# Two loads in the middle of a hybrid decoder block issued later, and one transposed tile evacuated earlier

## The chip, the cores and the metric

The kernel runs on one NeuronCore of a Trainium2 chip. The metric is the device time of one execution in microseconds. Before the change three runs took 972.06, 972.55 and 972.64 us, median 972.55 us. TensorE does the matrix products (PE in the profile, PEld its weight loads), VectorE and ScalarE the elementwise work (DVE, ACT), GpSimd a part of it (POOL). SyncE (SP; its instruction stream is SPq) issues most of the DMAs.

## The reference

One decoder block on 1024 tokens plus 16 meta tokens, width 1024, all in float32:

```
h   = concat(meta_tokens, x)
mix = mixer(rms_norm(h, pre_mix_norm))        # two causal convolution groups, then w_out
h   = h + rms_norm(mix, post_mix_norm)
xn  = rms_norm(h, pre_ffn_norm)
ff  = (silu(xn @ w_gate) * (xn @ w_up)) @ w_down     # 1024 -> 2816 -> 1024
out = (h + rms_norm(ff, post_ffn_norm))[16:]
```

The change lies where the mixer's output projection ends and the first products of `xn @ w_gate` and `xn @ w_up` begin.

## The kernel before

**Arithmetic.** A float32 operand is split into a rounded high part and the rest, its low part, and a product of two operands is made of three matmuls (`mm3`, lines 107 to 109: high by high, high by low, low by high; 512 columns each). So each matmul operand needs a cast on ACT (the high part) and a subtraction on DVE (the low part) before PE can use it.

**Output projection.** The mixer's output has eight row tiles of 128 tokens. `group` (quoted below) multiplies them by `w_out` in three groups: tiles 0 to 2, 3 to 5, then 6 and 7. Each group runs over the eight blocks of `w_out`, and between the blocks it calls the steps of a table, `at`. `norms` then makes of a group the new hidden state `h` (stored to DRAM as `hd`) and the normalised rows `hn`.

**Turning the tiles.** The FFN needs `hn` with channels on the partitions. Tiles 0 to 4 are turned by a DVE block transposition (`send`, line 675), a store to DRAM (`xd`, line 676), a load back in another order (`fetch`, line 681, four DMAs), and copies on ACT (`receive`, lines 689 to 691; `back(i)` calls it for tile i). Tiles 5, 6 and 7 are transposed on PE into two PSUM banks (`turn`, line 668, tile `pt`) and copied out by ACT (line 670). The result lies in four quadrants `raw`. `raw[0, 0]` holds tokens 0 to 511 and channels 0 to 511; its high and low parts are `B11h` and `B11l`, complete once tile 3 has been received.

**FFN.** The gate and up products are made in pairs (`Pair`) of weight blocks. A pair needs seven products of half size in place of eight; (j, n) is product n of pair j. The first ones are (0, 1), (1, 1), (0, 2), (1, 2), (0, 6), (1, 6), and (0, 1) and (1, 1) use `B11`, (j, 2) use `B21`, (j, 6) use `T2`. The weights of pair j arrive by `Pair.load` (line 746) in tiles `u`; in the program's full names `u110` is pair 1, up weights, first block. Their split parts are the tiles `op` (high: line 716 on ACT; low: line 703 on DVE). PSUM banks are handed out by hand: product (0, 1) takes banks 5 and 6, which the PE transposition of tile 5 used just before.

**What sets the order.** The whole program is ordered by hand: every engine executes in the order in which the source calls it, and SP issues its DMAs in that order too. A DMA that waits holds all DMAs behind it on SP. What it waits for is the data it moves, and the buffer it writes: `u110` lies in the ring `tp`, in the buffer that held `hn` of tile 5, so it may be loaded once PE has transposed tile 5. The other first blocks lie in the ring `wp`, in buffers that held blocks 5, 6 and 7 of `w_out` (tiles `ws_o`); these are free when DVE has made the low part of that block (line 168).

**Around the change.** During the group of tiles 6 and 7 the table calls `step1` to `step4` and, ahead of the last two blocks of `w_out`, `early`. `step1` calls `norms` for tiles 3 to 5 and sends tile 3, `step2` fetches it, `step3` sends tile 4, `early` receives tile 3, transposes tile 5 on PE and makes the operands of the products (0, 1) and (1, 1). `residual_x` (line 636) loads 128 rows of x, which `norms` adds for tiles 6 and 7.

Of the kernel before, what the change touches and what calls it, by code (L numbers as in the profile page):

```python
# [54 lines left out]
def hybrid_block(ctx: ExitStack, tc: tile.TileContext, xT, x, w_first, w_in, w_out, w_gate, w_up, w_down, par, g_post, g_ffn, g_out, out):  # L55
# [39 lines left out]
    def big(name, dt=F32R, pool=None):  # L95

        return (pool or xg).tile([P, 4 * HALF], dt, tag="x", name=name)
# [4 lines left out]
    def blocks(t):  # L102
        return t[:, : 4 * HALF].rearrange("p (a b) -> p a b", a=4)
# [52 lines left out]
    def split_o(k, eng=None):  # L156
        split_o_hi(k)
        split_o_lo(k, eng)

    def split_o_hi(k):  # L160
        if k in (3, 4):
            wu[k] = [held[k - 3][:, q, :] for q in range(2)]
        else:
            wu[k] = [wp.tile([P, D], F32R, tag=t, name=f"{t}_o{k}") for t in ("wh", "wl")]
        nc.scalar.copy(wu[k][0], raw_w["o", k])
# [468 lines left out]
    def residual_x(i):  # L634
        h = hp.tile([P, D], F32, tag="h", name=f"h{i}")
        nc.sync.dma_start(h, x[i * P : (i + 1) * P, :])
        return h

    def norms(grp, left, s1, hs, between=None, first=None, parts=False):
        n_ = len(grp)  # L640
        v = sm.tile([P, 16], F32, tag="s2", name=f"pm{grp[0]}")
        nc.vector.tensor_tensor(v[:, :n_], s1[:, 0:n_], s1[:, 4 : 4 + n_], op=ALU.add)
        r = rsqrt_n(v[:, :n_], 1.0 / D, RMS_EPS, n_, f"pm{grp[0]}")
        if first:
            first()
        v2 = sm.tile([P, 16], F32, tag="s2", name=f"pf{grp[0]}")
        n = {}
        for q, i in enumerate(grp):
            nc.vector.scalar_tensor_tensor(hs[i], left[i], r[:, q : q + 1], hs[i], op0=ALU.mult, op1=ALU.add)
            n[i] = row(tp, "t", f"hn{i}", TT)[:, :D]  # L650
            nc.scalar.activation(n[i], hs[i], AF.Square, accum_out=v2[:, q : q + 1])
            nc.sync.dma_start(hd[i], hs[i])
        if between:
            between()
        r = rsqrt_n(v2[:, :n_], 1.0 / D, RMS_EPS, n_, f"pf{grp[0]}")
        last = [lambda q=q, i=i: nc.vector.scalar_tensor_tensor(n[i], hs[i], r[:, q : q + 1], gB["ffn"], op0=ALU.mult, op1=ALU.mult) for q, i in enumerate(grp)]
        if parts:
            return n, last
        for f in last:
            f()  # L660
        return n

    def turn(i, n, at=(0, 1)):
        c = slice((i % 4) * P, (i % 4 + 1) * P)
        for q in range(2):
            pt = bank(at[q], f"pt{i}_{q}")
            for k in range(4):
                nc.tensor.transpose(pt[:, k * P : (k + 1) * P], n[:, (4 * q + k) * P : (4 * q + k + 1) * P], ident)
            p4 = pt.rearrange("p (a b) -> p a b", a=4)
            nc.scalar.copy(raw[q, i // 4][:, :, c], p4)  # L670
# [7 lines left out]
    def fetch(i, n):  # L678
        for j in range(4):
            src = xd[i].rearrange("(i r) (j x) -> j r i x", i=4, j=4)[j]  # L680
            nc.sync.dma_start(n[32 * j : 32 * j + 32].rearrange("r (i x) -> r i x", i=4), src)

    def receive(i, n):
        c = slice((i % 4) * P, (i % 4 + 1) * P)
        split4 = lambda t: t[:, :, c].rearrange("p k (i q) -> p k i q", i=4)
        for q in range(2):
            n4 = n.rearrange("p (i k q) -> p k i q", i=4, k=8)[:, 4 * q : 4 * q + 4]
            if q == 0 and i < 4:
                nc.scalar.copy(split4(B11[0]), n4)
                nc.vector.tensor_tensor(split4(B11[1]), n4, split4(B11[0]).bitcast(F32), op=ALU.subtract)  # L690
            nc.scalar.copy(split4(raw[q, i // 4]), n4)
# [10 lines left out]
    def sub(o, a, b, eng=None):  # L702
        (eng or nc.vector).tensor_tensor(o, a, b, op=ALU.subtract)  # L703
# [25 lines left out]
    class Pair:  # L729
# [19 lines left out]
        def a_side(self, n, m):  # L749
            a11, a12 = self.u[m, 0][:, :512], self.u[m, 0][:, 512:]  # L750
            if n not in (1, 2):
                a21, a22 = self.u[m, 1][:, :512], self.u[m, 1][:, 512:]
            if n == 1:
                s = a11
            elif n == 6:
                add(a21, a21, a22)
                sub(a11, a21, a11)
                s = a11
            elif n == 2:
                s = a12  # L760
            elif n == 5:
                s = a21
            elif n == 7:
                sub(a21, a22, a11)
                s = a21
            elif n == 3:
                sub(a12, a12, a11)
                s = a12
            else:
                s = a22  # L770
            return s
# [124 lines left out]
    hs = {i: residual_x(i) for i in (0, 1, 2)}  # L896
    pairs = {j: Pair(j) for j in range(3)}
# [10 lines left out]
    def turns(*grp, at=(0, 1)):  # L908
        return lambda: [turn(i, hn.pop(i), at if q or len(grp) == 1 else (0, 1)) for q, i in enumerate(grp)]

    def back(i):
        return lambda: receive(i, hn.pop(i))

    hs = {i: residual_x(i) for i in (3, 4, 5)}
# [57 lines left out]
    def turned(i):  # L972
        send(i, hn[i], big(f"xt{i}", F32, rp)[:, :D])
# [5 lines left out]
    def step1():  # L979
        n, muls = norms((3, 4, 5), left, s1, hs, between_5, lambda: split_o_hi(5), True)  # L980
        hn.update(n)
        pairs[1].load(0, (1,))
        muls[0]()
        turned(3)
        hn_muls.extend(muls[1:])
# [8 lines left out]
    def step3():  # L994
        split_o(7)
        pairs[1].load(0, (0,))
        turned(4)
        for i in (6, 7):
            hs[i] = residual_x(i)

    def step4():
        X[2] = pair("B21", (rp, rp))
# [2 lines left out]
    def b21_hi(c):  # L1005
        nc.scalar.copy(X[2][0][:, :, c], raw[1, 0][:, :, c])

    def b21_lo(c):
        sub(X[2][1][:, :, c], raw[1, 0][:, :, c], X[2][0][:, :, c].bitcast(F32))

    def early():
        for q in range(2):
            raw[q, 1] = blocks(big(f"raw{q}1", F32))
        a_side(0)
        b21_lo(slice(0, 3 * P))
        back(3)()
        b21_hi(slice(3 * P, 4 * P))
        b21_lo(slice(3 * P, 4 * P))
        turns(5, at=(5, 6))()
        fetch(4, hn[4])  # L1020
        a_side(1, (hp, "h"), (jp, "jk"))

    hn_muls = []
    s1, left = group((6, 7), up, {1: step1, 2: step2, 3: step3, 4: step4, 6: early})
    r11, r21, r12, r22 = raw[0, 0], raw[1, 0], raw[0, 1], raw[1, 1]
    T2r = blocks(big("T2r", F32))
# [404 lines left out]
```

## Time and profile before

| | |
|---|---|
| median of three runs | 972.55 us |
| the profiled execution: its own time | 972.49 us |
| its span (first to last instruction) | 970.7 us |
| mean granted TensorE clock | 0.993 |
| PE busy | 955.0 us, 98% |
| DVE busy | 713.6 us, 74% |
| ACT busy | 406.5 us, 42% |
| POOL busy | 249.6 us, 26% |

The difference between the execution's own time and its span, 1.8 us, lies around the instructions. PE is busy nearly throughout, so what is worth reading is where it is not. The views used below are the list of waits (who waited for whom, in total, how often, the longest), the chain of work that ended last, timelines of single engines (start, duration, what was done, and in brackets the idle time before it), tables by stretch with the granted clock, and the DMA issues with the time from issue to landing. Matmuls are pipelined: each row shows 0.39 us, but they start 0.23 us apart at the full clock.

### The profile page before, as it was taken

The numbers are of one execution on the slowest core, as the hardware profiler recorded it, in microseconds if no ns is written. First come the engines' busy times: TensorE is split into PE (matmuls) and PEld (weight loads), VectorE is DVE, ScalarE is ACT, GpSimd is POOL, SyncE is SP. The second block draws the span as 40 slices with busy tenths as digits, with TensorE's granted clock in tenths as the row PEclk, the third lists the DMA queues.
The fourth block names the chain that finished last, engine by engine and source line by source line (L and its number), as shares of the span: only waits on it lengthen the run. The fifth ranks groups of instructions, "written<-read, shape, count | busy, mean of one in ns | idle before, by whom it ended". The sixth has DMA issues, their size and how long they took to land.

```text
span 970.7 us, 12488 instructions
## 1 busy us (share of the span) xinstructions
PE 955.0 (98%) x4554; PEld 821.1 (85%) x4554; DVE 713.6 (74%) x1030; ACT 406.5 (42%) x666; POOL 249.6 (26%) x219
## 2 busy tenths in 40 slices
PE   9999999999999699999999999999999999999997
PEld 9999999998888588888888888888888888888885
DVE  7699999886467599997866876777765653546776
ACT  8533423465436473453443343443433333322341
POOL 1277945542000000004134132141240311112210
PEclk9999999999999799999999999999999999999999
DMA  8011111214356630464532623534319999866866
GB/s 309 23 44 63 47 44 44 65 44 163 121 180 231 211 115 1 184 241 161 217 131 109 238 109 131 187 127 163 147 31 343 321 329 376 261 186 200 321 209 245
DMA packets 62317, 161.92 MB, mean 167 GB/s; under 512 B 6576, under 2 KB 10160, under 8 KB 62256
## 3 DMA queue, kind: packets, MB, share of 16 engines
q1 hardware_dynamic: 45792, 109.08, 31.0%
q0 software_dynamic: 11088, 40.38, 12.9%
q10 hardware_dynamic: 5376, 11.67, 3.3%
q8 instruction: 36, 0.59, 0.3%
q14 instruction: 25, 0.20, 0.1%
HBM read 109.72 MB, written 51.38 MB: 166 GB/s over the span
## 4 chain that ended last, share of the span: by engine, by line
PE 98%; DMA 1%; ACT 0%; DVE 0%; SPq 0%; issue 0%; DVEq 0%; ACTq 0%
PE x L107 8%; PE x L109 8%; PE x L108 8%; PE y L107 6%; PE y L109 6%; PE y L108 6%; PE qx L109 4%; PE qx L108 4%; PE qx L107 4%; PE qy L108 3%; PE qy L109 3%; PE qy L107 3%; PE po L107 3%; PE po L109 3%; PE po L108 3%; PE p_v L108 2%
## 5 line engine op out<-in xcount | busy, mean ns | idle before, releaser
L716 ACT CAST op<-u 128x512 fp32r<-128x512 f32 x154 | 93.5, 622 | 190.4 <-DVE u L703 96.2
L703 DVE TENSOR_TENSOR op<-u,op 128x512 fp32r<-128x512 f32 x154 | 118.1, 808 | 48.6 <-ACT op L716 48.6
L703 DVE TENSOR_TENSOR db<-wb,db 128x512 fp32r<-128x512 f32 x77 | 54.9, 716 | 85.3 <-ACT db L1236 85.0
L706 POOL TENSOR_TENSOR C<-C,C 128x512 f32<-128x512 f32 x9 | 15.5, 1722 | 372.2 <-DMA gdA<-U 208.2
L1236 ACT CAST db<-wb 128x512 fp32r<-128x512 f32 x77 | 47.2, 620 | 116.3 <-PE qx L109 55.6
L108 PE MATMUL qx<-db,a 128*128 128x512 f32 x176 | 68.6, 390 | 0.0
L107 PE MATMUL qx<-db,a 128*128 128x512 f32 x176 | 68.6, 390 | 0.0
L109 PE MATMUL qx<-db,a 128*128 128x512 f32 x176 | 68.5, 389 | 0.0
L700 DVE TENSOR_TENSOR U<-y,U 128x512 f32<-128x512 f32 x66 | 43.1, 683 | 17.8 <-PE y L109 17.8
L108 PE MATMUL qy<-db,a 128*128 128x512 f32 x132 | 51.5, 390 | 0.0
L109 PE MATMUL qy<-db,a 128*128 128x512 f32 x132 | 51.4, 390 | 0.0
L107 PE MATMUL qy<-db,a 128*128 128x512 f32 x132 | 51.4, 390 | 0.0
L1109 POOL DMA_DIRECT2D a<-gdS x44 | 23.2, 528 | 91.6 <-PE qx L109 46.0
L706 POOL TENSOR_TENSOR U<-U,U 128x512 f32<-128x512 f32 x17 | 28.2, 1658 | 60.2 <-ACT U L831 46.5
L107 PE MATMUL x<-B11h,op 128*128 128x512 f32 x88 | 35.4, 402 | 8.0 <-ACT raw L670 8.0
L388 DVE SCALAR_TENSOR_TENSOR ae<-d,pr,ae 128x512 f32<-128x512 f32 x56 | 42.0, 750 | 0.0
L388 DVE SCALAR_TENSOR_TENSOR ac<-g,pr,ac 128x512 f32<-128x512 f32 x56 | 42.0, 750 | 0.0
L108 PEld LDWEIGHTS qx<-db,a 128*128 128x128 f32 x176 | 33.1, 188 | 6.9
L107 PEld LDWEIGHTS qx<-db,a 128*128 128x128 f32 x176 | 33.0, 188 | 6.9
L109 PEld LDWEIGHTS qx<-db,a 128*128 128x128 f32 x176 | 33.1, 188 | 6.8
L108 PE MATMUL x<-B11l,op 128*128 128x512 f32 x88 | 35.2, 400 | 0.0
L109 PE MATMUL x<-B11h,op 128*128 128x512 f32 x88 | 35.2, 400 | 0.0
(358 smaller groups left out, 2914.3 us busy)
## 6 DMA issues: line engine op xcount, KB each, us to landing
a<-gdS POOLq DMA_DIRECT2D x44, 512.0 KB, 4.0
a<-gdA POOLq DMA_DIRECT2D x33, 512.0 KB, 5.6
u<-w_gate_u SPq DMA_DIRECT2D x22, 512.0 KB, 4.9
u<-w_up_u SPq DMA_DIRECT2D x22, 512.0 KB, 5.8
gdS<-HI SPq DMA_DIRECT2D x44, 256.0 KB, 2.3
gdA<-HI SPq DMA_DIRECT2D x33, 256.0 KB, 2.0
gdS<-GS SPq DMA_DIRECT2D x33, 256.0 KB, 2.6
ws_o<-w_out_u SPq DMA_DIRECT2D x14, 512.0 KB, 4.6
```

The lines of the kernel that those rows point to most:

```text
L107: nc.tensor.matmul(o, lh, rh, start=start, stop=False, skip_group_check=again)
L108: nc.tensor.matmul(o, lh, rl, start=False, stop=False, skip_group_check=again)
L109: nc.tensor.matmul(o, ll, rh, start=False, stop=stop, skip_group_check=again)
L388: nc.vector.scalar_tensor_tensor(out if i == n - 1 else acc, src[:, i : i + HALF], w(i), init if i == first else acc, op0=ALU.mult, op1=AL ...
L700: (eng or nc.vector).tensor_tensor(o, a, b, op=ALU.add)
L703: (eng or nc.vector).tensor_tensor(o, a, b, op=ALU.subtract)
L706: (eng or nc.vector).tensor_tensor(o, a, b, op=ALU.mult)
L716: nc.scalar.copy(t[:, 0, :], src)
L1109: nc.gpsimd.dma_start(loads[n, j], gd[an][j])
L1236: nc.scalar.copy(t[:, 0, :], b)
```

## The change

Two issues on SP and two copies on ACT change places. No instruction is added, removed or resized.

- `pairs[1].load(0, (1,))`, the load of `u110`, goes from `step1` to `early`, behind the transposition of tile 5.
- The two loads of rows of x for tiles 6 and 7 go from `step3` to the place behind that.
- The transposition of tile 5 with its copies, `turns(5, ...)`, goes ahead of `back(3)`, which receives tile 3.

```
     def step1():
         n, muls = norms((3, 4, 5), left, s1, hs, between_5, lambda: split_o_hi(5), True)
         hn.update(n)
-        pairs[1].load(0, (1,))
         muls[0]()
...
     def step3():
...
         turned(4)
-        for i in (6, 7):
-            hs[i] = residual_x(i)
...
     def early():
...
         b21_lo(slice(0, 3 * P))
+        turns(5, at=(5, 6))()
+        pairs[1].load(0, (1,))
+        for i in (6, 7):
+            hs[i] = residual_x(i)
         back(3)()
         b21_hi(slice(3 * P, 4 * P))
         b21_lo(slice(3 * P, 4 * P))
-        turns(5, at=(5, 6))()
         fetch(4, hn[4])
         a_side(1, (hp, "h"), (jp, "jk"))
```

The DMAs on SP from the first weight load of pair 0 to the fetch of tile 4, before (u000, u010, u100, u110 are weight blocks: pair, gate 0 or up 1, block; xd3 and hn3 are tile 3 on its way to DRAM and back; h6 and h7 rows of x):

```order
L746 DMA u000_2862<-w_gate_u 128x1024
L746 DMA u110_2873<-w_up_u 128x1024
L676 DMA xd3_2262<-xt3_2876 128x1024
L746 DMA u010_2895<-w_up_u 128x1024
L681 DMA hn3_2850<-xd3_2262 32x4x256 x4
L746 DMA u100_2919<-w_gate_u 128x1024
L676 DMA xd4_2263<-xt4_2921 128x1024
L636 DMA h6_2924<-x_tok 128x1024
L636 DMA h7_2926<-x_tok 128x1024
L681 DMA hn4_2854<-xd4_2263 32x4x256 x4
```

The same DMAs after the change:

```order
L746 DMA u000_2862<-w_gate_u 128x1024
L676 DMA xd3_2262<-xt3_2874 128x1024
L746 DMA u010_2893<-w_up_u 128x1024
L681 DMA hn3_2850<-xd3_2262 32x4x256 x4
L746 DMA u100_2917<-w_gate_u 128x1024
L676 DMA xd4_2263<-xt4_2919 128x1024
L746 DMA u110_2982<-w_up_u 128x1024
L636 DMA h6_2984<-x_tok 128x1024
L636 DMA h7_2986<-x_tok 128x1024
L681 DMA hn4_2854<-xd4_2263 32x4x256 x4
```

Only u110 has moved, from second place to seventh; h6 and h7 stand behind xd4 as they did, now with u110 ahead of them.

ACT, from the operands of product (0, 1) to the first square of the group of tiles 6 and 7, before (pt5 is tile 5 in PSUM, op_1_jm the high parts for product (j, 1)):

```order
L716 CAST op_1_00_2969<-u000_2862 128x512
L716 CAST op_1_01_2971<-u010_2895 128x512
L689 CAST B11h_2552<-hn3_2850 128x4x128
L691 COPY raw00_2554<-hn3_2850 128x4x128
L691 COPY raw10_2555<-hn3_2850 128x4x128
L1006 CAST B21h_2940<-raw10_2555 128x4x128
L670 COPY raw01_2967<-pt5_0_2982 128x4x128
L670 COPY raw11_2968<-pt5_1_2988 128x4x128
L716 CAST op_1_10_2998<-u100_2919 128x512
L716 CAST op_1_11_3000<-u110_2873 128x512
L628 ACTIVATE sq60_3030,s1_6_3028<-po60_2818 128x512
```

After the change:

```order
L716 CAST op_1_00_2963<-u000_2862 128x512
L716 CAST op_1_01_2965<-u010_2893 128x512
L670 COPY raw01_2961<-pt5_0_2970 128x4x128
L670 COPY raw11_2962<-pt5_1_2976 128x4x128
L689 CAST B11h_2552<-hn3_2850 128x4x128
L691 COPY raw00_2554<-hn3_2850 128x4x128
L691 COPY raw10_2555<-hn3_2850 128x4x128
L1003 CAST B21h_2934<-raw10_2555 128x4x128
L716 CAST op_1_10_2998<-u100_2917 128x512
L716 CAST op_1_11_3000<-u110_2982 128x512
L628 ACTIVATE sq60_3030,s1_6_3028<-po60_2818 128x512
```

The two copies out of PSUM (L670) stand ahead of the four rows that receive tile 3. On PE, DVE and POOL the rows stand in the order in which they stood before.

More of the change, by code (lines that the diff above doesn't have):

```diff
@@ L981, in step1 @@
         hn.update(n)
-        pairs[1].load(0, (1,))
         muls[0]()
@@ L997, in step3 @@
         turned(4)
-        for i in (6, 7):
-            hs[i] = residual_x(i)
     def step4():
@@ L1015, in early @@
         b21_lo(slice(0, 3 * P))
+        turns(5, at=(5, 6))()
+        pairs[1].load(0, (1,))
+        for i in (6, 7):
+            hs[i] = residual_x(i)
         back(3)()
@@ L1018, in early @@
         b21_lo(slice(3 * P, 4 * P))
-        turns(5, at=(5, 6))()
         fetch(4, hn[4])
```

## The prediction

> **What bounds the kernel now.** PE is busy for 98% of the span, so I read its list of waits first (total us, how often, the longest):
>
> ```profile
> PE x L107 <- ACT raw L670: 8.0, 1, 8.0
> PE warm L89 <- DVE pr L113: 1.1, 1, 1.1
> ```
>
> The second is at the program's start. In the first, ahead of the first matmul of product (0, 1), PE stands for 8.0 us, and the copy of the transposed tile 5 out of PSUM releases it. The chain of work that ended last shows what led there (start, duration, what):
>
> ```profile
> 317.99 5.61 DMA xd<-xt
> ...
> 324.98 3.09 DMA hn<-xd
> 328.17 0.62 ACT B11h L689
> 328.79 1.05 ACT raw L691 x2
> 329.86 0.62 ACT B21h L1006
> 330.48 0.49 ACT raw L670
> 331.02 0.80 PE x L107
> ```
>
> Tile 3 leaves for DRAM at 317.99, comes back, and ACT receives it; only then does ACT copy tile 5, whose banks product (0, 1) takes. Tile 5 was transposed by 317.6, so its copy is late only because it stands behind tile 3 in ACT's order. Why tile 3 left so late is on SP, in its timeline and its waits from 307 to 326:
>
> ```profile
> 308.12 0.33 SPq L746 DMA_DIRECT2D u<-w_gate_u  x1
> 317.61 0.33 SPq L746 DMA_DIRECT2D u<-w_up_u  x1
> ...
> 318.51 0.38 SPq L746 DMA_DIRECT2D u<-w_up_u  x1
> 323.66 1.75 SPq L681 DMA_DIRECT2D hn<-xd  x4
> 325.51 0.38 SPq L746 DMA_DIRECT2D u<-w_gate_u  x1
> ```
> ```profile
> SPq L746 <- DVE hn L656: 6.8, 1, 6.8
> ...
> SPq L746 <- PE pt L668: 2.3, 1, 2.3
> ```
>
> After u000 (308.12) SP issues nothing until u110 at 317.61: 6.8 us until DVE has normalised tile 5, and 2.3 more until PE has transposed it, which frees u110's buffer. Behind u110 waits the store of tile 3, which DVE had ready long before:
>
> ```profile
> 310.48 1.25 DVE L675 STREAM_TRANSPOSE xt<-hn 128x1024 f32<-128x1024 f32 x1
> 311.65 1.18 DVE L168 TENSOR_TENSOR wl_o<-ws_o,wh_o 128x1024 fp32r<-128x1024 f32 x1
> ...
> 316.28 1.24 DVE L675 STREAM_TRANSPOSE xt<-hn 128x1024 f32<-128x1024 f32 x1
> ```
>
> Ready at 311.73, issued at 317.99: the stall begins there. Its price needs the last matmul ahead of it, the first of product (0, 2) behind it, 48 matmuls at full speed for comparison, and the clock (third number from the end of a stretch's row):
>
> ```profile
> 322.64 0.39 PE L109 MATMUL po<-wh_o,ybl 128*128 128x512 f32 x1
> ```
> ```profile
> L107 PE MATMUL x<-B21h,op x16: 389/390/479, 344.5 to 356.5; 128*128 128x512 f32 x16
> ```
> ```profile
> 400.66 0.39 PE L107 MATMUL x<-T4h,op 128*128 128x512 f32 x1
> ...
> 411.54 0.39 PE L107 MATMUL x<-B11h,op 128*128 128x512 f32 x1
> ```
> ```profile
> 324.00:326.00 2.00, 0.00 (x0) 0.00 (x0) 0.49 (x1) 0.62 (x1) 0.00 (x0) 1.00 0.48 154
> 326.00:328.00 2.00, 0.00 (x0) 0.00 (x0) 1.87 (x2) 0.00 (x0) 0.00 (x0) 0.51 0.98 207
> ...
> 336.00:338.00 2.00, 2.00 (x10) 1.60 (x9) 1.77 (x5) 1.69 (x5) 0.00 (x0) 0.93 0.04 11
> ```
>
> The 48 matmuls of (0, 4) and (1, 4) take 411.54 - 400.66 = 10.88 us, 0.227 each. So PE could begin (0, 1) at 322.64 + 0.23 = 322.87 and (0, 2), 48 matmuls later, at 333.75. It begins (0, 2) at 344.5. **The stall costs 10.75 us in all**: 331.02 - 322.87 = 8.15 of standing and 2.6 of matmuls at half clock until the clock is back at about 336.
>
> **The change, part by part.** First what tile 3 gains. The times from issue to landing, in the stretch 303 to 312, where one transfer follows another, and then in two busier ones (317 to 326, 325 to 336):
>
> ```profile
> hd<-h SPq DMA_DIRECT2D x3, 512.0 KB, 2.7
> u<-w_gate_u SPq DMA_DIRECT2D x1, 512.0 KB, 3.8
> ```
> ```profile
> xd<-xt SPq DMA_DIRECT2D x2, 512.0 KB, 5.9
> hn<-xd SPq DMA_DIRECT2D x4, 128.0 KB, 2.9
> ```
> ```profile
> h<-x_tok SPq DMA_DIRECT2D x2, 512.0 KB, 7.8
> ```
>
> And the making of B11's low part:
>
> ```profile
> 328.82 0.69 DVE L690 TENSOR_TENSOR B11l<-hn,B11h 128x512 fp32r<-128x512 f32 x1 [0.95 <-ACT B11h L689]
> ```
>
> *Tile 3's way.* With u110 out of the way SP issues the store at 311.8. It lands between 2.7 us later (the stores of h, also SBUF to DRAM) and 5.9 (the sends as they were, among loads): 314.5 to 317.7. I take 314.5, since only u010 goes out beside it; u010 waits for the low part of block 6, at 311.65 + 1.18 = 312.83, and lands at 316.7 (3.8) to 318.8 (5.9). The four fetches take SP 1.75 us, and the last, issued about 1.3 us behind the first, lands 2.9 us on: 314.5 + 1.3 + 2.9 = 318.7, at the slow end 321.9. ACT has the high part of product (0, 1) and its partner by then, and copies tile 5 out of PSUM ahead of tile 3, in time in which it would wait for tile 3. So B11h stands at 319.3 (318.7 + 0.62), the low part 0.7 later, at 320.0, against 322.87 when PE asks. *Without cover* the two copies would cost their 1.05 us. At the slow end B11h is ready at 322.5 and the low part at 323.2, needed by the second matmul at 323.1: a wait of 0.1. So the 8.15 us go, and with them the 2.6 of half clock.
>
> *What is late next: u110 itself.* SP reaches it behind the store of tile 4 (DVE ready at 316.28 + 1.24 = 317.52, 0.4 us to issue) at 318.0, 0.4 later than before, and it now stands behind u100 and that store. PE wants it only for the second half of (1, 1), at 322.87 + 36 x 0.227 = 331.0. But ACT works in order, and behind the cast of u110 stand the squares of tiles 6 and 7, which begin the whole normalisation; DVE follows ACT. These rows show the old times:
>
> ```profile
> 332.38 0.61 ACT L628 ACTIVATE sq<-po 128x512 f32<-128x512 f32 x1
> ...
> 340.91 1.05 ACT L803 COPY U<-x 128x512 f32<-128x512 f32 x2
> ...
> 353.61 1.22 ACT L930 CAST T2h<-T2r 128x512 fp32r<-128x512 f32 x2
> ```
> ```profile
> 355.30 1.29 DVE L703 TENSOR_TENSOR T2l<-T2r,T2h 128x512 fp32r<-128x512 f32 x2
> ```
> ```profile
> 357.14 1.98 PE L784 MATMUL y<-T2h,op 128*128 128x512 f32 x8
> 358.96 1.07 PE L784 MATMUL y<-T2l,op 128*128 128x512 f32 x4
> ```
>
> Product (0, 2) accumulates in the bank that the copy at 340.91 empties; half of its 1.05 us, 341.4, against 344.5 gives 3.1 us of room. Product (0, 6) needs the last T2h, at 353.61 + 1.22 = 354.83, at 357.14: 2.3 us, the tightest place; T2l, at 356.59, has 2.4. So PE can come forward by at most 2.3 us more than the ACT and DVE work does. That work comes forward by 332.38 less the new time of the first square, which is the landing of u110 plus 0.62 us of cast, and no earlier than 323.0, the end of PE's group.
>
> - u110 lands after 3.8 us (the load with the queue to itself), at 321.8: squares at 323.0, forward by 9.4, and PE gets all 10.75.
> - After 7.8 (the loads of x, which stood behind three transfers), at 325.8: squares at 326.4, forward by 6.0, PE by 8.3.
> - I take 5.9, the row of the sends, which also stood behind one or two transfers of that size: 323.9, squares at 324.5, forward by 7.9, PE by 7.9 + 2.3 = 10.2.
>
> *The rest costs nothing.* h6 and h7 go out at about 318.4 and 319; even after 7.8 us they are there at 326.8, when the four squares that begin at 324.5 end (0.6 each), and DVE adds them only after that. The fetch of tile 4 follows its store by itself. u010 and u100, issued at 318.5 and 325.5 before, come some 6 and 9 us earlier. If u010's landing were late, the cast of its part would hold the copies behind it; at 318.8 it is still ahead of tile 3's slow arrival.
>
> **Sum.** 972.49 (the profiled execution; the median of the runs, 972.55, is 0.06 above it) - 10.2 = **962.3 us**. Behind this stage PE works without a wait to the end, so an earlier PE ends earlier by as much.
>
> [...] The clock still stood at 1.00 in the stretch 324 to 326 and fell in the next, some 3 us into the wait. [...]
>
> **The rivals.**
>
> - *A late u110.* Its landing is at the far end or beyond, since the fetch of tile 3, u100, the store of tile 4 and it crowd the engines. For: loads of x took 7.8. Against: these stood among fetches of small pieces too. PE waits at (0, 2) or (0, 6), and gains 7.5 to 9.5: 963 to 965, about 964.3.
> - *Tile 3 is still late.* If store and fetch slow each other with u010, a part of the wait stays at 322.87. It does so once the fetch lands beyond 321.8 (0.62 + 0.69 ahead of 323.1); a rest of 3.2 us with half clock behind it costs 5.8 and leaves 4.9, 967.6. For: the sends took 5.9. Against: between 312 and 316 nothing else would be moving.
> - *The store does not move.* If something else than u110 held it, only ACT's order changes: PE starts after B11l, at 328.82 + 0.69 = 329.5 in place of 331.02, and the time is near 971.0. For: a store can wait for its own semaphore. Against: its data were ready at 311.73 and SP's waits name u110's buffer.
> - *Slower.* The order on ACT makes u110 the gate of the normalisation. Once it lands at 334.1 or later, the squares begin more than 2.3 us behind their old time and the gain is gone and more: landing at 336 puts them at 336.6, 4.2 behind, less the room of 2.3, and 1.9 is lost, 974.4. For: the gate is real. Against: 16 us in flight would be double the slowest transfer here.
>
> **How the numbers follow.** The forecast, 961.7 to 963, has 0.68; a late u110 0.16; a late tile 3 0.07; the unmoved store 0.05; slower 0.04. The range is 961.3 to 965.0: its low end is the whole 10.75 with 0.4 for the spread of runs (972.06 to 972.64), its high end takes in the late u110; some 0.15 is left out. A run tells 0.2%, 1.9 us, from no change. Faster by more than that: 0.68 + 0.16 + 0.07 = 0.91. Within: 0.05. Slower: 0.04.
>
> **What would show it.** The store of tile 3 on SP at 311.8; no wait of PE at (0, 1), or under 0.5 us; a clock of 1.00 from 324 on; (0, 2) at about 333.8; the first square between 323 and 325; and if PE waits anywhere, at (0, 2) or at (0, 6) for T2h, by some tenths. A wait of over 2 us at either, or SP silent until 317.6, would prove the forecast wrong.

## The result, and the profile after

| | before | after |
|---|---|---|
| median of the runs | 972.55 us (972.0 to 972.64) | 963.06 us (962.42 to 963.29) |
| the profiled execution: its own time | 972.49 us | 963.29 us |
| its span | 970.7 us | 961.5 us |
| mean granted TensorE clock | 0.993 | 0.999 |

The ratio after to before is 0.9903, with an interval of 0.9888 to 0.9917: 9.5 us faster, where 10.2 were forecast. The median is 0.8 us above the predicted time: inside the range of 961.3 to 965.0, and 0.06 above the upper end of the forecast's own 961.7 to 963, where the rival "A late u110" begins. One execution of the changed kernel, the profiled one of its repeat further down, ran at a granted clock of 0.851 and took 1054.83 us; it is left out of every comparison.

The list of PE's waits, whole (total us, how often, the longest):

```profile
PE warm L89 <- DVE pr L113: 1.1, 1, 1.1
PE p_g L108 <- DVE xl L185: 0.4, 1, 0.4
PE y L784 <- ACT T2h L930: 0.2, 1, 0.2
PE p_g L287 <- ACT xh L182: 0.2, 1, 0.2
```

The wait of 8.0 us ahead of product (0, 1) is gone. In this stage only the third row is left: 0.2 us ahead of (0, 6), for the last `T2h`; the two of `p_g` lie in the program's first 10 us. SP's timeline shows why the long wait is gone (start, duration, what):

```profile
311.89 0.32 SPq L676 DMA_DIRECT2D xd<-xt  x1
313.00 0.33 SPq L746 DMA_DIRECT2D u<-w_up_u  x1
314.70 1.75 SPq L681 DMA_DIRECT2D hn<-xd  x4
316.54 0.38 SPq L746 DMA_DIRECT2D u<-w_gate_u  x1
317.68 0.34 SPq L676 DMA_DIRECT2D xd<-xt  x1
318.11 0.86 SPq L746 DMA_DIRECT2D u<-w_up_u  x1
319.02 1.41 SPq L636 DMA_DIRECT2D h<-x_tok  x2
323.28 1.76 SPq L681 DMA_DIRECT2D hn<-xd  x4
```

Tile 3 leaves at 311.89 instead of 317.99, and u110 (the L746 row at 318.11) no longer stands ahead of it. PE's timeline has the last matmul of the output projection, the first of (0, 1), of (0, 2) and the last ahead of (0, 6), and the first of (0, 6):

```profile
323.16 0.39 PE L109 MATMUL po<-wh_o,ybl 128*128 128x512 f32 x1
323.39 0.39 PE L107 MATMUL x<-B11h,op 128*128 128x512 f32 x1
...
334.40 0.50 PE L107 MATMUL x<-B21h,op 128*128 128x512 f32 x1
...
347.13 0.39 PE L109 MATMUL x<-B21h,op 128*128 128x512 f32 x1
347.74 2.12 PE L784 MATMUL y<-T2h,op 128*128 128x512 f32 x8 [0.23 <-ACT T2h L930]
```

(0, 1) follows the projection without a gap. One thing has to be taken out of these times first. The projection now ends at 323.16, 0.52 us later than before (322.64), though nothing ahead of it changed; in the ten profiles compared here it ends between 322.64 and 323.78. So kernels are compared below by a stretch that starts there, from the last matmul of the projection to the first of (0, 6). **Before it is 357.14 - 322.64 = 34.50 us, after it 347.74 - 323.16 = 24.58**: 9.92 us are gained in the stage. Without any wait it would be 11.11 to (0, 2), as the prediction worked out (333.75 - 322.64), and from there the 12.64 of before (357.14 - 344.5): 23.75. The stage is 0.83 above that, more than the 0.23 of the row in brackets. That row counts from the end of the matmul ahead, 0.39 us behind its start, though the next one could start 0.23 behind it. By the starts, (0, 6) is 0.38 late (347.74 against 347.13 + 0.23), and (0, 2) is 0.13 late (334.40 against 323.39 + 10.88), for the copy that empties its bank; the other 0.32 lies behind that gap: the 24 matmuls of (0, 2) take 5.59 us (5.44 before), the 16 transpositions on PE 1.79 (1.66), and the 24 matmuls of (1, 2) 5.58 (5.54).

What is left shows on ACT, in its timeline, and in the chain that ended last, cut to this stage:

```profile
320.87 0.62 ACT L689 CAST B11h<-hn 128x512 fp32r<-128x512 f32 x1 [1.51 <-DVE B21l L703]
...
324.49 0.62 ACT L716 CAST op<-u 128x512 fp32r<-128x512 f32 x1 [0.79 <-DMA u<-w_up_u]
325.02 0.59 ACT L628 ACTIVATE sq<-po 128x512 f32<-128x512 f32 x1
...
330.31 1.15 ACT L691 COPY raw<-hn 128x512 f32<-128x512 f32 x2 [0.65 <-DMA hn<-xd]
...
346.47 1.22 ACT L930 CAST T2h<-T2r 128x512 fp32r<-128x512 f32 x2 [1.19 <-DVE T2r L703]
```
```profile
317.68 5.53 DMA xd<-xt
...
324.61 5.60 DMA hn<-xd
...
330.31 1.15 ACT raw L691 x2
...
346.47 1.23 ACT T2h L930 x2
...
347.74 1.43 PE y L784 x5
```

From 323 on ACT stands twice for a transfer: 0.79 us for u110, ahead of the squares, and 0.65 us for tile 4 coming back from DRAM (the L691 row). The chain ends on the second: store of tile 4, fetch, the copies, the normalised rows, `T2h`, PE. The prediction had followed u110 and counted tile 4 at nothing.

### The profile page after: what moved, and what is told of

The parts are those of the page before. It is cut to its first block, busy times and chain, and to the rows that moved or that the text cites. A ratio compares the mean times of both kernels' runs of the same rounds, so it can differ in the third digit from the quotient of the medians.

```text
span 961.5 us, 12487 instructions
## 1 busy us (share of the span) xinstructions
PE 952.9 (99%) x4554; PEld 818.9 (85%) x4554; DVE 713.5 (74%) x1030; ACT 406.5 (42%) x666; POOL 251.2 (26%) x219
## 4 chain that ended last, share of the span: by engine, by line
PE 93%; DVE 3%; DMA 2%; ACT 1%; issue 1%; SPq 0%; DVEq 0%; ACTq 0%
PE x L107 8%; PE x L109 8%; PE x L108 8%; PE y L107 6%; PE y L109 6%; PE y L108 6%; PE qx L108 4%; PE qx L109 4%; PE qx L107 4%; PE qy L108 3%; PE qy L109 3%; PE qy L107 3%; PE po L107 2%; PE po L109 2%; PE po L108 2%; PE p_c L107 2%
## 5 line engine op out<-in xcount | busy, mean ns | idle before, releaser
L107 PE MATMUL x<-B21h,op 128*128 128x512 f32 x88 | 34.5, 392 | 0.0
L109 PE MATMUL x<-B21h,op 128*128 128x512 f32 x88 | 34.3, 390 | 0.0
L108 PE MATMUL x<-B21l,op 128*128 128x512 f32 x88 | 34.3, 390 | 0.0
```

The source lines that it names most:

```text
L107: nc.tensor.matmul(o, lh, rh, start=start, stop=False, skip_group_check=again)
L108: nc.tensor.matmul(o, lh, rl, start=False, stop=False, skip_group_check=again)
L109: nc.tensor.matmul(o, ll, rh, start=False, stop=stop, skip_group_check=again)
```

## The experiments

Each of the eight variants stands beside the kernel before, timed on the same chip as it (median 973.15 us, for loads_sorted 973.33). Diffs are against the changed kernel. "Wait" is PE's longest in the stage; "half clock" is worked out from the rows by 2 us, as shown further down; "none" is a granted clock of 1.00 in every 2 us from 322 to 350 in the changed kernel, and in the five others matmuls that start 0.22 to 0.24 us apart, but for the first behind a gap or a transposition, in the rows looked at (322 to 334 and 346 to 358). The six kernels with ratios of 0.9895 to 0.9903 can't be told apart by their times: what is said of their differences rests on one profile of each, and how much the stretch of one kernel varies between profiles was not measured.

| kernel | stretch, us | wait, us | half clock, us | median, us | ratio (interval) |
|---|---|---|---|---|---|
| before | 34.50 | 8.0 at (0, 1) | 10.2 | | |
| changed kernel | 24.58 | 0.2 at (0, 6) | none | 963.06 | 0.9903 (0.9888 to 0.9917) |
| turn_only | 33.62 | 7.1 at (0, 1) | 6.8 | 971.31 | 0.998 (0.9972 to 0.9989) |
| loads_only | 24.91 | 0.4 at (0, 1) | none | 963.43 | 0.9898 (0.9885 to 0.9912) |
| x_rows_first | 29.04 | 3.4 at (1, 1) | 3.4 | 966.57 | 0.9932 (0.9919 to 0.9946) |
| up_last | 30.89 | 4.1 at (1, 1) | 6.8 | 968.39 | 0.9952 (0.9939 to 0.9964) |
| half_behind | 24.97 | 0.4 at (0, 2) | none | 963.35 | 0.9898 (0.9884 to 0.9913) |
| rows_behind | 25.03 | 0.4 at (0, 2) | none | 963.48 | 0.9901 (0.9887 to 0.9916) |
| all_three | 23.76 | none | none | 962.79 | 0.9896 (0.988 to 0.9913) |
| loads_sorted | 24.82 | 0.2 at (0, 6) | none | 963.42 | 0.9895 (0.9878 to 0.9911) |

### Which half of the change carries the gain

**turn_only** leaves the loads where they were and makes only the new order of tile 5 on ACT:

```
     def step1():
...
         hn.update(n)
+        pairs[1].load(0, (1,))
         muls[0]()
...
     def step3():
...
         turned(4)
+        for i in (6, 7):
+            hs[i] = residual_x(i)
...
         turns(5, at=(5, 6))()
-        pairs[1].load(0, (1,))
-        for i in (6, 7):
-            hs[i] = residual_x(i)
         back(3)()
```

> Kernel before, with the second half of the change alone: the transposition of tile 5 and its two copies ahead of the reception of tile 3, all loads at their old places. My theory (the store of tile 3 waits on SP behind u110, and that is the stall): the store still goes at about 318.0, PE still waits at product (0, 1), only until the low part of B11 (329.5 in place of 331.02), so 1.5 us less, and the squares come 1.0 us earlier: 970.5 to 971.3 us. Rival (the order on ACT carries the gain, since the copy of tile 5 released PE): 963 to 965 us.

SP's timeline and PE's waits of turn_only:

```profile
318.06 0.33 SPq L746 DMA_DIRECT2D u<-w_up_u  x1
318.45 0.42 SPq L676 DMA_DIRECT2D xd<-xt  x1
```
```profile
PE x L107 <- ACT B11h L689: 7.1, 1, 7.1
```

The store of tile 3 stays behind u110, and PE waits 7.1 us, now for `B11h` itself. This is the rival "The store does not move", worked out as a gain of 1.5 us. By the medians on this chip it is 1.84 (973.15 and 971.31), by the stretches of the two profiles 0.88; the runs of turn_only spread from 970.2 to 972.64.

**loads_only** does the other half: the loads move, the turn of tile 5 stays behind tile 3.

```
+        back(3)()
+        b21_hi(slice(3 * P, 4 * P))
+        b21_lo(slice(3 * P, 4 * P))
         turns(5, at=(5, 6))()
         pairs[1].load(0, (1,))
         for i in (6, 7):
             hs[i] = residual_x(i)
-        back(3)()
-        b21_hi(slice(3 * P, 4 * P))
-        b21_lo(slice(3 * P, 4 * P))
         fetch(4, hn[4])
```

> The changed kernel, with tile 5 transposed and copied behind the reception of tile 3 as in the kernel before: the moved loads alone. My theory: tile 3 is received from 320.9 on as in the changed kernel, the copies of tile 5 come at 323.1 to 324.1 behind it, so PE waits 0.3 us at product (0, 1) at about 323.4, its clock stays at 1.00, and the squares move by 0.2 us: 963.0 to 963.6 us, within 0.5 us of the changed kernel. Rival (the copies belong to the cause): PE stands for 1 us or more, 964.5 us or later.

PE's waits of loads_only in the stage:

```profile
PE x L107 <- ACT raw L670: 0.4, 1, 0.4
PE y L784 <- ACT T2h L930: 0.2, 1, 0.2
```

The wait for the copy of tile 5 is there again, but 0.4 us long instead of 8.0. The moved loads carry nearly all of the gain; the order on ACT is worth 24.91 - 24.58 = 0.33 us of the stretch, too little for the times to tell. That it is u110 among the moved loads, and not the rows of x, shows in x_rows_first below: there the rows keep their old place, and the wait at (0, 1) is gone all the same.

### Where a later u110 would bite

**x_rows_first** sends the two rows of x ahead of u110 again; **up_last** sends u110 behind the fetch of tile 4. In both u110 lands later and nothing else is added.

```
     def step3():
...
         turned(4)
+        for i in (6, 7):
+            hs[i] = residual_x(i)
...
         pairs[1].load(0, (1,))
-        for i in (6, 7):
-            hs[i] = residual_x(i)
```
```
         turns(5, at=(5, 6))()
-        pairs[1].load(0, (1,))
         for i in (6, 7):
             hs[i] = residual_x(i)
...
         fetch(4, hn[4])
+        pairs[1].load(0, (1,))
```

> The changed kernel, with the two loads of rows of x back at their old place, behind the store of tile 4 and so ahead of u110. My theory (the landing of u110 is the gate: ACT casts it ahead of the squares, DVE follows, PE waits at (0, 6) for T2h): u110 lands at 327 to 328.4 in place of 324.47, the squares begin that much later, 0.65 us of it is taken up by a wait for tile 4 that ACT has now, and PE waits 2 to 3 us more at (0, 2) to (0, 6): 965.0 to 966.5 us. Rival (ACT and DVE have room, and the wait of 0.2 us at (0, 6) has another cause): 963.1 us as the changed kernel.

> The changed kernel, with the load of u110 behind the fetch of tile 4 on SP. My theory: u110 is issued at about 325 and lands near 330, the squares begin near 330.8 in place of 325.0, 5.8 us later, less the 0.65 us that ACT now waits for tile 4, and PE loses about 5 us between (0, 1) and (0, 6): 967 to 969 us. Rival (u110 is wanted only by the second half of product (1, 1), at 331 on PE, so up to there its landing costs nothing): 963 to 963.5 us.

Timelines of ACT, of DVE and of PE in x_rows_first, then ACT's timeline in up_last and its waits of PE:

```profile
328.83 0.62 ACT L716 CAST op<-u 128x512 fp32r<-128x512 f32 x1 [4.58 <-DMA u<-w_up_u]
```
```profile
330.09 2.48 DVE L629 TENSOR_TENSOR jk<-po,gB_post 128x512 f32<-128x512 f32 x4
```
```profile
332.03 0.50 PE L107 MATMUL x<-B11h,op 128*128 128x512 f32 x1 [3.35 <-DVE jk L629]
```
```profile
330.49 0.62 ACT L716 CAST op<-u 128x512 fp32r<-128x512 f32 x1 [6.51 <-DMA u<-w_up_u]
```
```profile
PE x L107 <- DVE jk L629: 4.1, 1, 4.1
```

ACT stands 4.58 and 6.51 us for u110, and PE then stands 3.4 and 4.1 us. So u110 is a real gate. The times came out near what was expected (966.57, just beyond 965.0 to 966.5, and 968.39, within 967 to 969), but in part by luck, since the path is another: PE does not wait at (0, 2) or (0, 6). It waits at (1, 1), for DVE's L629 (`jk`). The program hands out PSUM banks by a list, and (1, 1) takes 7 and 4, where tile 7's projection lies (`OUT_BANKS`) until DVE has multiplied it out; DVE does this behind the low part of u110's operand. In the changed kernel L629 runs from 325.75, and three of its four pieces of 0.62 us, the ones that empty bank 7, are done at 327.6. (1, 1) begins 24 matmuls behind 323.39, at 328.83. **So (1, 1) has 1.2 us left in the changed kernel, a gate that the prediction had not looked at.** It did not bite there, and it is not the first to bite: in loads_sorted below, with squares 0.9 us later against the projection than in the changed kernel, PE waits 0.2 us each at (0, 2) and (0, 6) and not at (1, 1). A longer delay meets it. The sizes agree: against 23.75 the two stretches lose 5.3 and 7.1 us. Of this 3.4 and 4.1 are standing, and half of the matmul time at half clock makes another 1.7 (3.4 / 2) and 2.9 ((339.5 - 333.7) / 2); some 0.2 is left in each.

### What is the gate now

The changed kernel once more, on the chip of the next three kernels:

> The changed kernel itself once more, beside the three variants of it that follow: about 0.990 of the kernel before on the same chip; squares at about 325.0, a wait of some tenths at (0, 6) for T2h.

The ratio is again 0.9903 (0.9886 to 0.9919). What was expected of the squares and of (0, 6) is not confirmed by it, since its only profile is that of the execution left out above.

**half_behind** takes u110 out from ahead of the squares: its operand is made behind them, at the start of `first`.

```
         fetch(4, hn[4])
-        a_side(1, (hp, "h"), (jp, "jk"))
+        half(0)
+
+    def half(m):
+        src = pairs[1].a_side(1, m)
+        t = operand_hi(src, f"1_1{m}", ((hp, "h"), (jp, "jk"))[m])
+        sub(t[:, 1, :], src, t[:, 0, :].bitcast(F32))
+        made.setdefault(1, []).append(t)
...
-    results = {s: pairs[order[s][0]].product(order[s][1], made.pop(s)) for s in range(2)}
+    results = {0: pairs[0].product(1, made.pop(0))}
...
     def first():
+        half(1)
+        results[1] = pairs[1].product(1, made.pop(1))
```

> The changed kernel, with the second half of the operands of product (1, 1), those of u110, made behind the squares instead of ahead of them. Theory A (the landing of u110 is the one gate of ACT, so PE's last wait at (0, 6) follows it): squares at 323.7 in place of 325.0, T2h up to 1.2 us earlier, PE without a wait at (0, 6), 0.6 to 0.9 us faster than the changed kernel. Theory B (behind u110 stands a second gate, tile 4, whose fetch lands at 330.2 and for which ACT waits 0.65 us in the changed kernel): the squares come earlier, ACT then waits about 1.5 us for tile 4, T2h stays within 0.2 us, and so does the time. I hold with B.

ACT's timeline of half_behind:

```profile
330.44 1.15 ACT L691 COPY raw<-hn 128x512 f32<-128x512 f32 x2 [1.23 <-DMA hn<-xd]
```

The squares start 1.06 us behind the projection (323.96 - 322.90) instead of 1.86, and nothing comes of it: ACT now stands 1.23 us for tile 4 instead of 0.65, and the stretch is no shorter (24.97 against 24.58). u110 alone is not the gate of the changed kernel.

**rows_behind** lets the fetch of tile 4 pass the rows of x:

```
-        for i in (6, 7):
-            hs[i] = residual_x(i)
         back(3)()
...
         fetch(4, hn[4])
+        for i in (6, 7):
+            hs[i] = residual_x(i)
```

> The changed kernel, with the two loads of rows of x behind the fetch of tile 4. Theory B: the fetch lands at 327 to 328, ACT receives tile 4 without its wait of 0.65 us, T2h comes 0.4 to 0.65 us earlier, and the time is 0.3 to 0.6 us less than that of the changed kernel; the rows land at 329 to 330.5, just when DVE adds them. Theory A (u110 the only gate; its landing is the same): the same time as the changed kernel.

DVE's timeline of rows_behind, and ACT's:

```profile
330.08 2.48 DVE L649 SCALAR_TENSOR_TENSOR h<-jk,r_pm,h 128x1024 f32<-128x1024 f32 x2 [0.73 <-DMA h<-x_tok]
```
```profile
331.40 1.06 ACT L651 ACTIVATE hn<-h 128x1024 f32<-128x1024 f32 x1 [0.56 <-DVE h L649]
```

The wait for tile 4 is gone, and one for the rows of x takes its place: DVE stands 0.73 us, ACT 0.56 behind it. The stretch is no shorter, which was not expected. Nor did u110 land as before: it was issued at 318.58, and the squares start 2.24 us behind the projection (325.15 - 322.91) instead of 1.86.

**all_three** makes both edits and also sends pair 1's first gate block (u100) behind the store of tile 4:

```
     def step3():
         split_o(7)
-        pairs[1].load(0, (0,))
...
-        pairs[1].load(0, (1,))
-        for i in (6, 7):
-            hs[i] = residual_x(i)
+        pairs[1].load(0)
...
         fetch(4, hn[4])
-        a_side(1, (hp, "h"), (jp, "jk"))
+        for i in (6, 7):
+            hs[i] = residual_x(i)
+        half(0)
```

> Both of these together, with u100 behind the store of tile 4, so that this store goes ahead of it. If u110 and tile 4 are the two gates, neither holds ACT now: squares at about 323.8, tile 4 received without a wait, T2h 1.2 us earlier, no wait of PE at (0, 2) to (0, 6): 0.8 us less than the changed kernel, which is all that is left of the 10.75 us. If a third thing holds DVE or ACT, the time is that of rows_behind or later.

ACT's timeline of all_three and its PE waits, whole:

```profile
328.68 1.14 ACT L691 COPY raw<-hn 128x512 f32<-128x512 f32 x2
...
345.11 1.23 ACT L930 CAST T2h<-T2r 128x512 fp32r<-128x512 f32 x2 [1.18 <-DVE T2r L703]
```
```profile
PE warm L89 <- DVE pr L113: 1.1, 1, 1.1
```

Tile 4's copies start without a wait, the last `T2h` is there 0.8 us before PE asks (345.11 + 1.23 = 346.34 against 347.18), and no wait of PE is left in the stage: the stretch of 23.76 is the 23.75 of a stage without waits. In time this is 0.8 us at most, and the intervals overlap: it can't be told from the changed kernel.

**loads_sorted** keeps SP's order of all_three without the split of the operands, to see whether u110 still gates once tile 4 and the rows do not:

```
         b21_lo(slice(3 * P, 4 * P))
         fetch(4, hn[4])
         for i in (6, 7):
             hs[i] = residual_x(i)
-        half(0)
+        a_side(1, (hp, "h"), (jp, "jk"))
...
```

(This diff alone is against all_three. Behind the mark the lines of half_behind go back to those of the changed kernel.)

> The kernel all_three without its split of the operands: SyncE's order of all_three (store of tile 4, first up weights of pair 1, u110, fetch of tile 4, the rows h6 and h7), and ACT's order of the changed kernel (u110's operand ahead of the squares). If u110 no longer gates anything by itself (theory B, since only the fetch of tile 4 and the rows stood behind the wait at product (0, 6)), the stretch from the last matmul of the output projection to the first of (0, 6) is that of all_three, 23.77 us, with no wait of PE there, and the squares come 1.6 us or less after PE's first matmul of (0, 1). If u110 still gates (theory C), the squares come 1.5 to 2 us after that matmul, the last T2h after PE is free, and PE waits 0.2 to 0.5 us at (0, 6), so that the stretch is 24.0 to 24.3. In time both lie within 0.5 us of the changed kernel, a ratio to the kernel before of 0.989 to 0.991.

The chain of loads_sorted in this stage:

```profile
319.45 6.10 DMA u<-w_up_u
325.57 0.63 ACT op L716
...
330.75 1.04 ACT raw L691 x2
...
348.19 1.88 PE y L784 x7
```

u110 gates: the chain runs through it, and tile 4's copies follow ACT's own work. The size was missed by half a microsecond: with u100 ahead of it u110 is issued at 319.45 instead of 318.11, the squares start 2.5 us behind the first matmul of (0, 1) instead of 1.5 to 2, and the stretch is 24.82 instead of 24.0 to 24.3. So three arrivals stand within about a microsecond of each other here: u110, tile 4 and the rows of x. Of the orders tried, each that favours one leaves another late, and only all_three, which also takes u110's operand out of the way of the squares, loses all its waits.

## Why the prediction was right, and where it was off

**The cause and the stall's price: right.** The stall went with the move of u110 (loads_only) and not with the order on ACT (turn_only), nor does it need the rows of x moved (x_rows_first). The price of 10.75 us in the profile of before is confirmed by all_three, whose stretch is 34.50 - 23.76 = 10.74 shorter.

**Tile 3's way: right in effect, one term too short.** The store was forecast at 311.8 and left at 311.89; its fetch could be issued at 314.70, 2.8 us later (forecast 2.7). `B11h` was forecast complete at 319.3 and was complete at 321.49, 1.7 later when the later end of the projection, 0.52, is taken off. The term that was too short is the landing of the fetches, 2.9 us. From issue to landing the four took 4.0 in the median, and the last, issued at 316.0, took 4.8: it landed at 320.8, and ACT began its cast at 320.87. The issues of the changed kernel from 311 to 320, then rows of DVE and of ACT in all_three:

```profile
hn<-xd SPq DMA_DIRECT2D x4, 128.0 KB, 4.0
```
```profile
319.36 1.75 DVE L703 TENSOR_TENSOR B21l<-raw,B21h 128x1536 fp32r<-128x1536 f32 x1
```
```profile
320.57 0.62 ACT L689 CAST B11h<-hn 128x512 fp32r<-128x512 f32 x1 [0.96 <-DMA hn<-xd]
```

The bracket at 320.87 in the changed kernel's timeline names DVE's `B21l`, which ended in the same moment. But the cast does not wait for it: in all_three ACT begins it at 320.57, and DVE is at `B21l` until 321.11. The longer landing cost nothing: the low part, begun at 321.52 and 0.69 long, stood at 322.21, against 323.39.

**u110: right, by two small errors that cancel.** It was issued at 318.11 (forecast 318.0, so 0.4 early when the 0.52 is taken off) and took 6.4 us (forecast 5.9). The squares began 1.86 us behind the last matmul of the projection. Before it was 9.74, so this work came forward by 7.88, forecast 7.9.

**The mis-sized step: "The rest costs nothing ... The fetch of tile 4 follows its store by itself".** From the first square to tile 4's copies ACT took 5.06 us before (332.38 to 337.44, with a wait of 0.31 for tile 4 in it) and 5.29 after (325.02 to 330.31, with 0.65). From there to the last `T2h` it is 16.17 and 16.16. So 0.22 were lost, all on the way to tile 4. Before, in ACT's timeline and in SP's:

```profile
337.44 1.15 ACT L691 COPY raw<-hn 128x512 f32<-128x512 f32 x2 [0.31 <-DMA hn<-xd]
```
```profile
325.99 0.38 SPq L676 DMA_DIRECT2D xd<-xt  x1
326.41 1.60 SPq L636 DMA_DIRECT2D h<-x_tok  x2
332.31 1.75 SPq L681 DMA_DIRECT2D hn<-xd  x4
```

ACT stood 0.31 us for tile 4 already then, so there was no room in that place, and whatever the fetch gained less than the squares had to be lost. The store went forward by 8.3 us (325.99 to 317.68) and the copies by 7.1, or 7.65 counted from the end of the projection, against 7.88 of the squares: u110, the store and the two rows of x stand close together ahead of the fetch, which takes 5.60 us from its last issue in the chain above. The room at (0, 6) gave 2.26 of its 2.31, since PE began 0.05 us behind the end of `T2h` (346.47 + 1.22 = 347.69). So the stage gained 7.88 - 0.22 + 2.26 = 9.92 instead of 10.2.

**The remaining 0.7 us** between the stage's 9.92 and the profiled executions' 9.20 (972.49 - 963.29) lies outside it: 0.52 in the later end of the projection, and 0.2 behind (0, 6), where the span has 613.76 us left after and 613.56 before. Nothing there was changed. The 0.52 is there long before the stage: PE's first product with `wh_b` starts at 120.4 before and at 121.0 after, its last at 233.9 and 234.4, and PE's list after has the two waits for `p_g` at the program's start, 0.6 us in all, that the list before lacks. Of the 0.2, 0.14 is the wait's own wake: behind it the first eight matmuls of (0, 6) take 2.12 us, before 1.98.

**The room: right where it looked, and one gate missed.** The prediction looked at (0, 2) and (0, 6), and there a slightly late u110 does show: by tenths in the changed kernel and in loads_sorted. It did not look at (1, 1), which inherits a PSUM bank from the projection and has 1.2 us left in the changed kernel. At the landing on which the rival "A late u110" was priced this alters little: squares at 326.4 would be 1.9 us later than the changed kernel's (324.5 with the 0.52 taken off), so PE would wait 1.9 - 1.2 = 0.7 at (1, 1) and by as much less at (0, 6). In x_rows_first and up_last, with squares 4.7 and 5.4 us later than the changed kernel's, it decides alone: PE has no wait at (0, 2) or (0, 6) left, and half clock comes on top (1.7 and 2.9 us).

**The other rivals.** "A late u110" has the median by 0.06 us, but not by its signs: u110 took 6.4 us, nearer to the forecast's 5.9 than to the rival's 7.8 or more, and PE waits 0.2 us. Its gain of 8.3 us counts the wait that it leaves, 10.75 - 8.3 = 2.45 us, at its own length; that no half clock comes on top was the author's estimate, which no run shows: PE's waits here were of 1.1 us at most or of 3.4 and more, and the one of 3.4 cost 1.7 more. Of the 1.0 us that the profiled execution is short of the forecast gain of 10.2, 0.3 lies in the stage and 0.7 outside it. "Tile 3 is still late" did not come about, as PE's list of waits shows. "The store does not move" is excluded by SP's row at 311.89. "Slower" needed u110 at 334 or later; even in up_last it is there at 330.5, and that kernel is still 0.5% faster than before.

**What would have shown it wrong** was a wait of over 2 us at (0, 2) or (0, 6). The only one in the stage is the 0.2 us at (0, 6); (0, 2) began at 334.40, which is 333.88 with the 0.52 taken off, against 333.8 forecast.

## What the runs showed of the hardware

**Half clock lasted 3.4, 6.8, 6.8 and 10.2 us in the four profiles that have it.** Granted clock by 2 us (third number from the end) where it falls and comes back, in x_rows_first and then in up_last:

```profile
332.00:334.00 2.00, 1.97 (x6) 0.70 0.00 0
...
336.00:338.00 2.00, 2.00 (x10) 0.95 1.05 420
```
```profile
332.00:334.00 2.00, 0.32 (x1) 0.68 0.00 0
...
338.00:340.00 2.00, 2.00 (x7) 0.62 1.06 395
```

The stretches beside these read 1.00 ahead of the fall (330 to 332) and 0.50 behind it (334 to 336), and at 0.50 the matmuls start 0.43 us apart. With these two values a mean of 0.70 over 2 us is 0.8 us at full and 1.2 at half clock, so in x_rows_first the clock fell at 332.8 and came back at 336.2: 3.4 us of half clock. By the same working it was 6.8 us in up_last (332.7 to 339.5), 6.8 in turn_only (328.7 to 335.6, from 0.68 in 328 to 330 and 0.61 in 334 to 336) and 10.2 before (326.0 to 336.3, from 0.51 in 326 to 328 and 0.93 in 336 to 338): one, two, two and three times 3.4. The fall came 3.0 to 5.2 us after PE's last row ended; in x_rows_first PE had been at work again for 0.8 us by then. The return came 4.2 to 5.8 us after PE resumed. What sets the two moments was not shown. By this working the wait of 3.4 us cost 1.7 us more than itself and the one of 4.1 us 2.9 more. Behind the wait of 0.2 us in the changed kernel the clock read 1.00 (346 to 350), and behind the one of 0.4 us in loads_only the matmuls started 0.22 to 0.23 us apart from the second on. No profile has a wait of PE between 1.1 and 3.4 us.

**The same load takes 4.5 to 8.9 us.** u110, 512 KB each time, took from its issue to the cast that waited for it 8.9 us in x_rows_first (issued at 319.90, behind u100, the store of tile 4 and both rows of x), 6.4 in the changed kernel (318.11, behind u100 and the store), 6.1 in loads_sorted and 4.5 in up_last (325.94, behind everything else of the stage). Not all of this is the place in SP's order: loads_only, whose order is that of the changed kernel, has 7.1 (issued at 318.25, cast at 325.36). The prediction's bounds, 3.8 to 7.8, held for the order that they were made for, and would not hold for that of x_rows_first.

## What to carry to other kernels

A load that had to wait for its buffer held every transfer behind it on SP here, among them a store that was ready 6.3 us earlier. Look for data that was ready long before its store left, and move the waiting load back behind it. When one gate goes, list every arrival that the next engine in order needs, with its lateness against that engine (here u110, tile 4 and the rows of x within a microsecond), and every PSUM bank that the next matmuls inherit: a longer delay can meet a gate that was not on the old chain, as (1, 1) was not. A wait of 0.2 us left PE's clock at 1.00 here; the four of 3.4 to 8.0 us also paid half clock, for 3.4 to 10.2 us.
